# Moving the last weight preparations from GpSimd to VectorE around the start of the up-projection

## The chip, the cores and the metric

The kernel runs on one core of a Trainium2 chip. A core has five engines that work side by side, each through its own instructions in order: TensorE multiplies matrices (PE in the profile, PEld for its weight loads), VectorE (DVE) and GpSimd (POOL) do elementwise arithmetic, ScalarE (ACT) does activations and copies, and SyncE (SP) issues most DMA transfers; ScalarE and GpSimd can issue transfers too. On-chip memory is SBUF; TensorE writes its sums into the banks of PSUM. The metric is the device time of one execution in microseconds (us); lower is better.

## The reference

One layer of a decoder trunk on a sequence of 1024 rows of width 1024, in float32. Three branches (RWKV-7 time mixing, stick-breaking attention, cross-attention) are gated, summed and projected; a convolutional feed-forward block follows. Only the end of it matters here:

```python
branch_out = jnp.einsum('btnc,ncd->btnd', ys, w_branch[l])
gates = jax.nn.sigmoid(gate_logits.reshape(b, t, N_BRANCH, D_MODEL))
merged = jnp.sum(gates * branch_out, axis=2)
x = x + merged @ w_out[l]
x = x + conv_ffn(x, norm2_g[l], w_up[l], conv_w[l], conv_b[l], w_down[l])

def conv_ffn(x, g, w_up, conv_w, conv_b, w_down):
    h = rms_norm(x, g) @ w_up                      # 1024 -> 2 * 2816
    hp = jnp.pad(h, ((0, 0), (CONV_W - 1, 0), (0, 0)))
    acc = conv_b + hp[:, 0:t] * conv_w[0]
    for i in range(1, CONV_W):
        acc = acc + hp[:, i:i + t] * conv_w[i]     # causal, width 3
    gate, val = jnp.split(acc, 2, axis=-1)
    return (jax.nn.silu(gate) * val) @ w_down
```

## The kernel before, in words

**Split operands.** Each float32 operand x of a large product is split into a high part, which ScalarE writes by a rounding copy, and a low part x - high, written by an elementwise subtraction on VectorE or GpSimd. A product is then three matmuls: high by high, high by low, low by high. Whoever needs an operand waits for both parts.

**End of the branches and output projection.** `branch_last` computes the last branch in eight steps d of 128 output columns. In each, TensorE fills two PSUM banks, VectorE multiplies them by the gate (line 1230, which frees the banks), adds the sums of the other branches (line 1235), ScalarE writes the high parts `mg` (line 1241) and VectorE their low parts (line 1242). Then `out_proj` multiplies by the eight rows of tiles of the output weights, `wo[0]` to `wo[7]`, for eight blocks `tt` of 128 rows; blocks 0 and 1 run together, one k after the other. `load_wo(k)` loads and splits `wo[k]`: 0 to 3 inside `branch_last`, 4 to 7 at the start of `out_proj`, their low parts on GpSimd (line 85). The raw weights use two buffers `wr`, so `wo[6]` is loaded when `wo[4]` is split. In SBUF the parts of `wo[4]` are called `it` and `wo_sp`, those of 5 and 6 `qk`, of 7 `at`.

**Up-projection.** The activations are cut into four blocks of 512 by 512, and the product with the weights follows a scheme with seven products and sums of blocks in place of eight. The left operands, prepared once for all weights, are called 11 and 21 (`B` in the profile), 22 (also `B`), and T1 to T4 (`BT`). The weights come in pairs of 128-column tiles; pair 0 is a pair of gate columns, pair 1 the value columns that belong to it, and so on, 22 pairs. For pair n, product i (1 to 7) is 12 matmuls of 128x512 into one of four `mm` banks. The weights' operands are prepared per pair: `prep1` (products 1 and 2) from the first tile, `prep2` (5 and 6) from the sum s that `sums2` makes, `prep3` (7, 4 and 3) from the two that `sums3` makes. In the profile s is `it`, the raw tiles are `rw` (odd pairs) or `wr` (even ones), and the operands are `wh`, `wl` (high, low) and `l`. For pair 0 they come early, during the output projection (`wsec`, `wsum`, `wsh`, `wsl`). After the products VectorE combines the banks into `u`, and `conv` computes the convolution and the activation into `gall` (instructions on ScalarE and VectorE in turn), whose sums `act_sums` writes out for the down-projection.

**What sets the order.** A scheduler orders the instructions of an engine by priority and by what they wait for, and allots buffers; nothing moves once the program is built. `pinned` keeps instructions of one engine in the order of the code while `pin` is on; while `strict` is on too, each is also tied behind the pinned one before it. All matmuls are pinned. `behind(ins, prev)` ties one instruction behind another. In the up phase `strict` was off, and the order at its start is a list of calls: `step(n, i)` is product i of pair n, `hi` and `lo` write parts of left operands, `late(7)` transposes the last block of rows, `sums` makes the left operands' sums.

Of the kernel before, what the change touches and what calls it, by code (L numbers as in the profile page):

```python
# [12 lines left out]
F32 = mybir.dt.float32  # L13
# [8 lines left out]
C = 64  # L22
# [28 lines left out]
class Trunk:  # L51
# [30 lines left out]
    def split_raw(self, raw, hi, lo):  # L82
        ins = self.nc.scalar.activation(hi, raw, AF.Copy)  # L83
        self.behind(ins, self.last_fin)
        self.nc.gpsimd.tensor_tensor(lo, raw, hi.bitcast(F32), ALU.subtract)  # L85
        return hi, lo
# [1101 lines left out]
    def load_wo(self, k):  # L1188
        slots = ["qk"] * 4 + ["at"] * 4 + ["it", "sp"] + ["qk"] * 4 + ["at"] * 2
        hl = [self.pool_l.tile([128, 1024], F32R, name="wo_sp", tag="sp", bufs=1) if s == "sp" else self.t4(s, F32R) for s in slots[2 * k : 2 * k + 2]]  # L1190
        self.wo.append(self.split_raw(self.load_w(self.I["w_out"][k], self.last_go if k > 3 else None), *hl))
# [201 lines left out]
    def up_phase(self, raws, t2, operand, high, low, late, sums):  # L1393
# [13 lines left out]
        def load(n):  # L1407
            if n < len(pairs):
# [3 lines left out]
                for i in range(2):  # L1412
                    nc.sync.dma_start(W[n][i], self.I["w_up"][m + i])
# [10 lines left out]
        def prep1(n):  # L1424
            w = self.early[4 * n] if n < 2 else hl(W[n][0], self.pool_wt, ("wh", "wl"))
            st[n, 1], st[n, 2] = [[x[:, c] for x in w] for c in (L, R)]

        def sums2(n):
            keep = self.pinned if n == 1 else lambda ins: None
            w1, w2 = W[n]  # L1430
            s = st[n, "s"] = self.t4("it")
            keep(nc.gpsimd.tensor_tensor(s[:, L], w2[:, L], w2[:, R], ALU.add))
            keep(nc.gpsimd.tensor_tensor(s[:, R], s[:, L], w1[:, L], ALU.subtract))

        def sums3(n):
            keep = self.pinned if n == 1 else lambda ins: None
            w1, w2 = W[n]
            s4 = st[n, "s4"] = self.pool_r.tile([128, 552], F32, name=self.nm("s4"), tag="s4", bufs=1)[:, :512]
            keep(nc.gpsimd.tensor_tensor(w2[:, L], w1[:, L], w2[:, L], ALU.subtract))
            keep(nc.gpsimd.tensor_tensor(s4, w1[:, R], st[n, "s"][:, R], ALU.subtract))  # L1440

        def prep2(n):
            if n > 1:
                sums2(n)
            w = hl(st[n, "s"], self.pool_l, ("l4", "l4"), fixed=n < 2) if n else self.early[1]
            st[n, 5], st[n, 6] = [[x[:, c] for x in w] for c in (L, R)]

        def prep3(n):
            if n > 1:
                sums3(n)  # L1450
            w = hl(W[n][1] if n else self.early[2], self.pool_wt, ("wh", "wl"), fixed=n < 2, eng=nc.gpsimd if n else nc.vector)
            st[n, 7], st[n, 4] = [[x[:, c] for x in w] for c in (L, R)]
            if n:
                W.pop(n)
                del st[n, "s"]
                st[n, 3] = hl(st.pop((n, "s4")), self.pool_l, ("l4", "l4"), 512, n == 1)
# [23 lines left out]
        def conv_half(n, i, u, sg, h):  # L1480
            m = pairs[n][0] + i
            c = self.ps("g")
            nc.scalar.activation(c, u[:, 2 + h * 512 : 514 + h * 512], AF.Identity, scale=self.par("cw2", m), bias=self.par("cb", m))
            nc.vector.scalar_tensor_tensor(c, u[:, 1 + h * 512 : 513 + h * 512], self.par("cw1", m), c, ALU.mult, ALU.add)
            nc.vector.scalar_tensor_tensor(c, u[:, h * 512 : 512 + h * 512], self.par("cw0", m), c, ALU.mult, ALU.add)
            g = g_all[:, i * 2 + h]
            if not pairs[n][2]:
                nc.scalar.activation(sg[:, h], c, AF.Sigmoid)
                nc.vector.tensor_tensor(g, c, sg[:, h], ALU.mult)
            else:  # L1490
                nc.vector.tensor_tensor(g, c, g, ALU.mult)

        def conv(n, i, u):
            sg = None if pairs[n][2] else self.pool_l.tile([128, 2, 512], F32, name=self.nm("sg"), tag="sp", bufs=1)
            for h in range(2):
                conv_half(n, i, u, sg, h)
# [15 lines left out]
        def step(n, i):  # L1512
            if i == 1:
                A = st[n, "A"] = bank()
                product(n, 1, A, True, True)
                p1 = st[n, "p1"] = self.r4("p1", n=512)
                if n < 2:
                    self.pinned(nc.vector.tensor_copy(p1, A))  # L1518
                else:
                    nc.scalar.activation(p1, A, AF.Copy)  # L1520
# [8 lines left out]
            elif i == 6:  # L1529
# [5 lines left out]
                if n and pairs[n - 1][2]:  # L1535
                    act_sums(pairs[n - 1][1], True)
            elif i == 7:
# [8 lines left out]
                nc.vector.tensor_tensor(v[:, L2], Bk, st.pop((n, "p1")), ALU.add)  # L1546
                nc.vector.tensor_tensor(v[:, R2], st[n, "C"], v[:, L2], ALU.add)
# [13 lines left out]
            elif i == 3:  # L1561
# [6 lines left out]
                if n + 1 == len(pairs):  # L1568
                    conv(n, 1, st.pop((n, "u2")))
                conv(n, 0, u)  # L1570
# [13 lines left out]
        self.pin = True  # L1584
# [3 lines left out]
        step(0, 1)  # L1588
        sums2(1)
        hi("T1", old)  # L1590
        lo("T1", old)
        step(1, 1)
        sums3(1)
# [361 lines left out]
```

## Time and profile before

| | |
|---|---|
| time, median of 3 runs | 1824.77 us (1822.93 to 1825.58) |
| profiled execution, its own time | 1822.09 us |
| its span, first to last instruction | 1820.3 us |
| mean granted TensorE clock | 0.996 |
| output projection on TensorE | 1079.6 to 1177.4 us of the span |
| up-projection | from 1177.6 us |

A row of the timeline is: start in us, duration in us, engine, line, operation, out<-in, shape, a count where like instructions were merged, and in brackets the idle time of the engine ahead of it with what ended it. Merged instructions overlap a little, so two of 0.69 us each show as 1.3. A row of the waits is: engine and line that waited, engine and line waited for, us in total, times, the longest. In the answer by windows: stretch, its length, then busy us of PE, PEld, VectorE, ScalarE and GpSimd, the granted clock (1.00 is full), the DMA share and GB/s. In the groups by shape, the numbers after the bar are the busy us of all and the mean ns of one.

### The profile page before, as it was taken

Reading aid. Unit: us, or ns where it says so; the run is one execution under the profiler, and the core shown is the slowest. Engines: PE = TensorE matmul, PEld = TensorE weight load, DVE = VectorE, ACT = ScalarE, POOL = GpSimd, SP = SyncE. Lnnn points to the kernel's source line nnn. Section 1 sums busy time; section 2 is a strip of 40 time slices with the busy share of each in tenths; the row PEclk is TensorE's granted clock in tenths of the full one; section 3 lists DMA queues with packets and bytes.
Section 4 is the critical chain, followed back from the end, with each engine's and each line's share of the span. In section 5 each row is a group of like instructions: output and inputs, shape, how many; then the busy total and the mean of one; then the engine's idle time right before and its main releaser. Section 6 shows DMA issues by size and latency. Waiting matters only on the chain.

```text
span 1820.3 us, 27424 instructions
## 1 busy us (share of the span) xinstructions
PE 1784.4 (98%) x10468; PEld 1444.0 (79%) x10468; DVE 1191.1 (65%) x1659; ACT 882.7 (48%) x1665; POOL 770.1 (42%) x441
## 2 busy tenths in 40 slices
PE   8999999999999999999999999989999999999999
PEld 6777778878888888787777878868888888888887
DVE  5657773988977515232634792597776777786497
ACT  5443352555666645543556543464444444544343
POOL 2322343222221362221333341476777767645454
PEclk9999999999999999999999999999999999999999
DMA  4155466111112352457864562323332333386475
GB/s 182 59 174 185 146 191 221 50 42 50 58 41 79 103 162 65 154 190 243 283 230 182 204 213 105 127 61 113 110 110 87 101 114 110 122 298 240 145 236 203
DMA packets 120613, 263.39 MB, mean 145 GB/s; under 512 B 28313, under 2 KB 40857, under 8 KB 120354
## 3 DMA queue, kind: packets, MB, share of 16 engines
q1 hardware_dynamic: 82722, 194.76, 32.6%
q10 hardware_dynamic: 33984, 54.27, 8.1%
q0 software_dynamic: 3776, 12.62, 2.2%
q8 instruction: 82, 1.34, 0.3%
q14 instruction: 49, 0.40, 0.1%
HBM read 180.04 MB, written 81.53 MB: 144 GB/s over the span
## 4 chain that ended last, share of the span: by engine, by line
PE 77%; DVE 12%; issue 4%; ACT 3%; POOL 2%; DMA 2%; ACTq 0%; SPq 0%; DVEq 0%; POOLq 0%
PE mm L130 63%; PE g L130 11%; PE g L113 3%; POOL dw L1687 1%; DVE it L479 1%; DVE at L872 1%; DVE inst L481 1%; DVE qk L396 1%; DVE qk L398 1%; DVE BT L1328 1%; DVE w L774 0%; DVE qk L819 0%; DVE at L1235 0%; DMA w<-mrd 0%; DVE qk L606 0%
## 5 line engine op out<-in xcount | busy, mean ns | idle before, releaser
L85 POOL TENSOR_TENSOR wl<-wr,wh 128x1024 fp32r<-128x1024 f32 x77 | 195.7, 2542 | 443.5 <-ACT wh L83 437.0
L130 PE MATMUL mm<-xhi,wh 128*128 128x512 f32 x784 | 263.3, 416 | 8.3 <-ACT xhi L199 7.3
L130 PE MATMUL mm<-xlo,wh 128*128 128x512 f32 x784 | 245.5, 395 | 0.9 <-DVE xlo L200 0.9
L130 PE MATMUL mm<-xhi,wl 128*128 128x512 f32 x784 | 243.6, 392 | 0.0
L130 PEld LDWEIGHTS mm<-xlo,wh 128*128 128x128 f32 x784 | 148.2, 189 | 34.5 <-DVE xlo L200 1.6
L130 PEld LDWEIGHTS mm<-xhi,wl 128*128 128x128 f32 x784 | 147.9, 189 | 33.8 <-POOL wl L85 0.9
L130 PEld LDWEIGHTS mm<-xhi,wh 128*128 128x128 f32 x784 | 137.1, 190 | 38.3 <-issue 8.8
L83 ACT ACTIVATE wh<-wr 128x1024 fp32r<-128x1024 f32 x77 | 81.5, 1059 | 91.4 <-PE mm L130 51.3
L130 PE MATMUL mm<-dw,da 128*128 128x512 f32 x528 | 120.8, 390 | 0.0
L130 PE MATMUL mm<-BT,l 128*128 128x512 f32 x504 | 117.7, 389 | 0.0
L130 PEld LDWEIGHTS mm<-dw,da 128*128 128x128 f32 x528 | 98.9, 188 | 21.3 <-DVE da L1686 0.8
L1687 POOL TENSOR_TENSOR dw<-draw,dw 128x512 fp32r<-128x512 f32 x55 | 82.3, 1505 | 77.4 <-ACT dw L1685 75.9
L130 PE MATMUL mm<-BT,wh 128*128 128x512 f32 x352 | 109.2, 390 | 2.9 <-DVE BT L1328 2.9
L130 PEld LDWEIGHTS mm<-BT,l 128*128 128x128 f32 x504 | 94.6, 188 | 19.6
L130 PE MATMUL mm<-B,wh 128*128 128x512 f32 x352 | 108.6, 390 | 1.5 <-DVE p L1518 1.5
L872 DVE TENSOR_TENSOR_SCAN at<-at,at 128x128 f32<-128x128 f32 (+3 forms) x64 | 90.0, 1407 | 27.9 <-ACT at L866 27.7
L1686 DVE TENSOR_TENSOR da<-draw,da 128x512 fp32r<-128x512 f32 x77 | 70.6, 928 | 47.6 <-ACT da L1684 47.2
L1419 POOL TENSOR_TENSOR l<-it,l 128x1024 fp32r<-128x1024 f32 x21 | 51.6, 2457 | 95.5 <-ACT l L1418 95.5
L130 PE MATMUL g<-dw,da 128*128 128x512 f32 x396 | 90.5, 389 | 0.3 <-POOL dw L1687 0.3
L1684 ACT ACTIVATE da<-draw 128x512 fp32r<-128x512 f32 x77 | 48.3, 628 | 82.9 <-PE mm L130 32.0
L774 DVE TENSOR_TENSOR w<-w,rbc 128x1024 f32<-128x1024 f32 x24 | 50.5, 2105 | 58.0 <-ACT w L773 54.7
L186 POOL TENSOR_TENSOR hf<-rs,half 128x16 f32<-128x16 f32 (+1 forms) x18 | 48.9, 2718 | 91.1 <-DVE rs L183 86.4
(329 smaller groups left out, 4021.3 us busy)
## 6 DMA issues: line engine op xcount, KB each, us to landing
wr<-in_w_in_dram SPq DMA_DIRECT2D x50, 512.0 KB, 3.6
draw<-actd SPq DMA_DIRECT2D x77, 256.0 KB, 3.5
at<-scr SPq DMA_DIRECT2D x28, 512.0 KB, 5.4
draw<-in_w_down_dram SPq DMA_DIRECT2D x55, 256.0 KB, 4.7
rw<-in_w_up_dram SPq DMA_DIRECT2D x22, 512.0 KB, 3.5
actd<-gall ACTq DMA_DIRECT2D x44, 256.0 KB, 3.4
gsd<-w ACTq DMA_DIRECT2D x20, 512.0 KB, 2.8
wr<-in_w_up_dram SPq DMA_DIRECT2D x20, 512.0 KB, 3.7
```

Source lines behind the costliest of these rows:

```text
L83: ins = self.nc.scalar.activation(hi, raw, AF.Copy)
L85: self.nc.gpsimd.tensor_tensor(lo, raw, hi.bitcast(F32), ALU.subtract)
L113: self.pinned(self.nc.tensor.transpose(out, in_, self.ident[:n, :n]))
L130: self.pinned(self.nc.tensor.matmul(*a, **k))
L186: nc.gpsimd.tensor_tensor(out, t[:, :n], self.half[:, :n], ALU.pow)
L396: nc.vector.tensor_tensor(bk4[q, :, first ^ h2], self.c8(x[q, hs]), self.c8(Q[q, hs]), ALU.mult)
L774: nc.vector.tensor_tensor(g, g, self.rbc, ALU.mult)
L872: self.pinned(nc.vector.tensor_tensor_scan(sn[:, :W][:, ::-1], sn[:, :W][:, ::-1], self.smask[:, 1024 - W :][:, ::-1], 1.0, ALU.mult, ALU. ...
L1419: keep(eng.tensor_tensor(lo, src, hi.bitcast(F32), ALU.subtract))
L1684: self.pinned(nc.scalar.activation(A[:, 0], a, AF.Copy))
L1686: self.pinned(nc.vector.tensor_tensor(A[:, 1], a, A[:, 0].bitcast(F32), ALU.subtract))
L1687: nc.gpsimd.tensor_tensor(Wt[:, 1], w, Wt[:, 0].bitcast(F32), ALU.subtract)
```

## The change

Two things are changed, both between 1070 and 1250 us of the span.

*Output weights.* The low parts of `wo[4]` to `wo[7]` are written by VectorE, tied behind the last pinned VectorE instruction, that is behind the low parts of `branch_last`'s last step.

*Up phase up to the third pair.* `sums2`, `sums3` and the low parts of pairs 0 and 1 run on VectorE instead of GpSimd. The two copies `p` of product 1 out of PSUM run on ScalarE instead of VectorE. The low parts of T1, T3 and 22 are written in one instruction of 1024 elements per half instead of 768 and 256. Products of pair 2: product 1 stands ahead of product 3 of pair 1. Its raw weights are loaded by ScalarE's queue, behind the high part of s of pair 1, instead of SyncE's. The second convolution of pair 0 (on `u`), the convolutions of pair 1 and the sums of the first activations come later in the code, the two halves of pair 0's convolutions are interleaved, and the order up to pair 1's product 7 is strict.

The list of calls at the start of the up phase, and what it calls, from the diff:

```diff
-    def split_raw(self, raw, hi, lo):
+    def split_raw(self, raw, hi, lo, dve=False):
         ins = self.nc.scalar.activation(hi, raw, AF.Copy)
         self.behind(ins, self.last_fin)
-        self.nc.gpsimd.tensor_tensor(lo, raw, hi.bitcast(F32), ALU.subtract)
+        if dve:
+            ins = self.nc.vector.tensor_tensor(lo, raw, hi.bitcast(F32), ALU.subtract)
+            self.behind(ins, self.last_fixed[ins.ins.engine])
+        else:
+            self.nc.gpsimd.tensor_tensor(lo, raw, hi.bitcast(F32), ALU.subtract)
...
-        self.wo.append(self.split_raw(self.load_w(...), *hl))
+        self.wo.append(self.split_raw(self.load_w(...), *hl, k > 3))
...
-                    nc.sync.dma_start(W[n][i], self.I["w_up"][m + i])
+                    if n == 2:
+                        self.pinned(nc.scalar.dma_start(W[n][i], self.I["w_up"][m + i]))
+                    else:
+                        nc.sync.dma_start(W[n][i], self.I["w_up"][m + i])
...
+        def engine(n):
+            return self.pinned if n < 3 else lambda ins: None, nc.vector if n < 2 else nc.gpsimd
...
+                ins = nc.scalar.activation(p1, A, AF.Copy)
                 if n < 2:
-                    self.pinned(nc.vector.tensor_copy(p1, A))
...
-        self.pin = True
+        self.pin = self.strict = True
         load(1)
         prep1(0)
         prep1(1)
         step(0, 1)
+        step(1, 1)
         sums2(1)
-        hi("T1", old)
-        lo("T1", old)
-        step(1, 1)
-        sums3(1)
         late(7)
+        hi("T1", old)
...
+        prep2(1)
+        load(2)
         step(0, 7)
-        prep2(1)
+        sums3(1)
         u = step(0, 3)
-        prep3(1)
-        load(2)
         v = step(0, 4)
...
+                if n == 1 and i == 4:
+                    step(2, 1)
+                elif n == 2 and i == 6:
+                    conv(1, 0, u)
+                    act_sums(0, False)
+                elif n == 2 and i == 7:
+                    act_sums(0, True)
+                if n == 1 and i == 6:
+                    prep3(1)
+                    prep1(2)
+                    conv(0, 1, v)
+                elif n == 1 and i == 7:
+                    conv(0, 0, u)
+                    self.strict = False
```

VectorE where the output projection starts; `mg` are the last low parts of `branch_last`, `w<-mm,w` is the first sum of the output projection. Before:

```order
L1242 TENSOR_TENSOR mg_1_3_9599<-at_9897,mg_0_3_9595 128x512
L1242 TENSOR_TENSOR mg_1_0_1_9605<-at_9897,mg_0_0_1_9601 128x256
L1242 TENSOR_TENSOR mg_1_1_1_9607<-at_9897,mg_0_1_1_9603 128x256
L1276 TENSOR_TENSOR w_1653_10113<-mm_10007,w_1653_10113 128x512
L1276 TENSOR_TENSOR w_1653_10113<-mm_10008,w_1653_10113 128x512
```

After, in the changed kernel, whose lines are four further on here:

```order
L1246 TENSOR_TENSOR mg_1_3_9599<-at_9897,mg_0_3_9595 128x512
L1246 TENSOR_TENSOR mg_1_0_1_9605<-at_9897,mg_0_0_1_9601 128x256
L1246 TENSOR_TENSOR mg_1_1_1_9607<-at_9897,mg_0_1_1_9603 128x256
L86 TENSOR_TENSOR wo_sp<-wr_9978,it_9976 128x1024
L86 TENSOR_TENSOR qk_9983<-wr_9984,qk_9982 128x1024
L86 TENSOR_TENSOR qk_9989<-wr_9990,qk_9988 128x1024
L86 TENSOR_TENSOR at_9995<-wr_9996,at_9994 128x1024
L1280 TENSOR_TENSOR w_1653_10113<-mm_10007,w_1653_10113 128x512
```

The four low parts of the output weights stand between the two, where GpSimd had them at its own pace.

VectorE at the start of the up phase, from the sum of product 6 of pair 0 on (`BT...10724` is T3, `B...10728` is 22, the next `BT` T4). Before:

```order
L1534 TENSOR_TENSOR u_10825<-mm_10845,p_1728_10750 128x512
L1328 TENSOR_TENSOR BT_1_0_10726<-A_10001,BT_0_0_10724 128x2x384
L1328 TENSOR_TENSOR BT_1_1_10727<-A_10002,BT_0_1_10725 128x2x384
L1328 TENSOR_TENSOR BT_1_0_10726<-A_10001,BT_0_0_10724 128x2x128
L1328 TENSOR_TENSOR BT_1_1_10727<-A_10002,BT_0_1_10725 128x2x128
L1419 TENSOR_TENSOR wl_10864<-wsec_10509,wh_10863 128x1024
L1328 TENSOR_TENSOR B_1_0_10730<-A_10003,B_0_0_10728 128x1024
L1328 TENSOR_TENSOR B_1_1_10731<-A_10004,B_0_1_10729 128x1024
L1328 TENSOR_TENSOR BT_1_0_10873<-raw_10000,BT_0_0_10871 128x1024
L1328 TENSOR_TENSOR BT_1_1_10874<-raw_10000,BT_0_1_10872 128x1024
L1542 TENSOR_TENSOR u_10888<-mm_10845,p_1728_10750 128x512
```

After:

```order
L1546 TENSOR_TENSOR u_10820<-mm_10840,p_1728_10750 128x512
L1332 TENSOR_TENSOR BT_1_0_10726<-A_10001,BT_0_0_10724 128x1024
L1426 TENSOR_TENSOR wl_10856<-wsec_10509,wh_10855 128x1024
L1332 TENSOR_TENSOR BT_1_1_10727<-A_10002,BT_0_1_10725 128x1024
L1332 TENSOR_TENSOR B_1_0_10730<-A_10003,B_0_0_10728 128x1024
L1426 TENSOR_TENSOR l_1742_10880<-wsum_10510,l_1741_10879 128x512
L1332 TENSOR_TENSOR B_1_1_10731<-A_10004,B_0_1_10729 128x1024
L1332 TENSOR_TENSOR BT_1_0_10886<-raw_10000,BT_0_0_10884 128x1024
L1332 TENSOR_TENSOR BT_1_1_10887<-raw_10000,BT_0_1_10885 128x1024
L1426 TENSOR_TENSOR l_1744_10893<-it_10767,l_1743_10892 128x1024
L1554 TENSOR_TENSOR u_10876<-mm_10840,p_1728_10750 128x512
```

Two low parts `l` have joined from GpSimd, and `wl` stands between the halves of T3; further on (not shown) follow `sums3` of pair 1 and its two last low parts.

GpSimd at the start of the up phase (`rs` is the last row norm). Before:

```order
L186 TENSOR_TENSOR rs_1723_10707<-rs_10710,half 128x1
L1432 TENSOR_TENSOR it_10752<-rw_10734 128x512
L1433 TENSOR_TENSOR it_10752<-it_10752,rw_10733 128x512
L1439 TENSOR_TENSOR rw_10734<-rw_10733,rw_10734 128x512
L1440 TENSOR_TENSOR s_1732_10774<-rw_10733,it_10752 128x512
L1419 TENSOR_TENSOR l_1743_10892<-wsum_10510,l_1742_10891 128x512
L1419 TENSOR_TENSOR l_1745_10914<-it_10752,l_1744_10913 128x1024
L1419 TENSOR_TENSOR wl_10931<-rw_10734,wh_10930 128x1024
L1432 TENSOR_TENSOR it_11013<-wr_10939 128x512
```

After:

```order
L190 TENSOR_TENSOR rs_1723_10707<-rs_10710,half 128x1
L1426 TENSOR_TENSOR wl_10967<-wr_10896,wh_10966 128x1024
L1442 TENSOR_TENSOR it_11000<-wr_10897 128x512
L1443 TENSOR_TENSOR it_11000<-it_11000,wr_10896 128x512
L1426 TENSOR_TENSOR l_1764_11004<-it_11000,l_1763_11003 128x1024
L1449 TENSOR_TENSOR wr_10897<-wr_10896,wr_10897 128x512
```

GpSimd's first instruction of the up phase is now the low part `wl` of pair 2, and the eight that belonged to pairs 0 and 1 are gone.

92 lines of the change are left out of this document (49 added, 43 removed).

## The prediction

> **What bounds the kernel now.** I read the busy times first, then who TensorE waited for, then the timeline at each of those waits.
>
> ```profile
> PE 1784.4 (98%) x10468; PEld 1444.0 (79%) x10468; DVE 1191.1 (65%) x1659; ACT 882.7 (48%) x1665; POOL 770.1 (42%) x441
> ```
>
> TensorE is the bound over the whole. The same number of matmuls stays, so only its gaps can be won. Its waits from 960 to 1250 us, which holds all the change touches, but for one of 0.5 us in the branches:
>
> ```profile
> PE mm L130 <- DVE BT L1328: 2.9, 2, 1.7
> PE mm L130 <- DVE at L1230: 2.3, 1, 2.3
> PE mm L130 <- DVE p L1518: 1.5, 1, 1.5
> PE mm L130 <- DVE u L1547: 1.1, 1, 1.1
> PE mm L130 <- DVE wl L1419: 1.0, 1, 1.0
> ```
>
> Together 8.8 us, all ended by VectorE. Behind them TensorE has no gap to take a gain back:
>
> ```profile
> 1235.00:1300.00 65.00, 65.00 (x289) 53.83 (x288) 44.20 (x67) 31.22 (x43) 49.79 (x30) 1.00 0.28 94
> 1300.00:1400.00 100.00, 100.00 (x443) 82.84 (x442) 77.85 (x115) 47.23 (x65) 73.63 (x43) 1.00 0.35 115
> ```
>
> TensorE is busy for 65 of 65 and 100 of 100 us, GpSimd for about three quarters, so what is won ahead of 1235 us reaches the end unless GpSimd or VectorE falls behind there.
>
> **Gap one, where the output projection starts.** The timeline of three engines:
>
> ```profile
> 1076.34 2.40 POOL L85 TENSOR_TENSOR wo_sp<-wr,it 128x1024 fp32r<-128x1024 f32 x1 [9.56 <-ACT it L83]
> 1076.60 4.95 DVE L1242 TENSOR_TENSOR mg<-at,mg 128x256 fp32r<-128x256 f32 x2 [0.55 <-ACT mg L1241]
> 1078.70 2.56 POOL L85 TENSOR_TENSOR qk<-wr,qk 128x1024 fp32r<-128x1024 f32 x1
> 1079.63 1.52 PE L130 MATMUL mm<-qk,mg 128*128 128x512 f32 x6
> 1082.68 1.28 DVE L1230 TENSOR_TENSOR at<-mm,at 128x512 f32<-128x512 f32 x2
> 1083.41 6.34 PE L130 MATMUL mm<-qk,mg 128*128 128x512 f32 x18 [2.26 <-DVE at L1230]
> 1089.60 5.60 PE L130 MATMUL mm<-at,mg 128*128 128x512 f32 x24
> ...
> L1328 DVE TENSOR_TENSOR BT<-t,BT 128x256 fp32r<-128x256 f32 x2 | 0.8, 423 | 0.1
> ```
>
> Two subtractions of 256 elements took 4.95 us where the last row has 0.42 us for each: they end with GpSimd's two subtractions `wo_sp` and `qk` (1078.7 and 1081.3). An instruction of VectorE that reads two operands from SBUF has waited here for a whole one of GpSimd, twice. Behind them stand the sums (1.3 us) and then the gate product of line 1230 that frees the banks for block 1. TensorE sat idle for 2.26 us.
>
> It cost more than that. 24 matmuls take 5.60 us in the last PE row, a pitch of (5.60 - 0.39) / 23 = 0.227 us with 0.39 us for the last one. The 18 behind the gap lasted from 1083.41 to 1089.60, 6.19 us, where 18 x 0.227 = 4.08: 2.11 us more, since the granted clock fell to one half.
>
> ```profile
> 1085.00:1087.00 2.00, 2.00 (x6) 1.62 (x5) 2.00 (x1) 1.06 (x1) 2.00 (x1) 0.50 0.00 0
> ```
>
> The clock took its price here after a gap of 2.26 us. [...]
>
> **Gap two, the start of the up phase.**
>
> ```profile
> 1183.03 0.86 PEld L113 LDWEIGHTS g<-kon,sq 128*128 128x128 f32 x8 [0.25 <-ACT sq L1286]
> 1183.75 3.94 DVE L1328 TENSOR_TENSOR BT<-raw,BT 128x768 fp32r<-128x768 f32 x2 [0.77 <-ACT BT L1323]
> 1188.35 0.73 PE L130 MATMUL mm<-B,wh 128*128 128x512 f32 x2 [1.47 <-DVE p L1518]
> 1197.13 1.22 DVE L1419 TENSOR_TENSOR wl<-wsec,wh 128x1024 fp32r<-128x1024 f32 x1
> 1198.41 0.51 PE L130 MATMUL mm<-BT,wl 128*128 128x512 f32 x1 [0.97 <-DVE wl L1419]
> 1200.95 3.03 POOL L1419 TENSOR_TENSOR l<-it,l 128x1024 fp32r<-128x1024 f32 x1 [1.44 <-ACT l L1418]
> 1201.65 6.74 DVE L1328 TENSOR_TENSOR BT<-raw,BT 128x1024 fp32r<-128x1024 f32 x2
> 1203.94 3.37 POOL L1419 TENSOR_TENSOR wl<-rw,wh 128x1024 fp32r<-128x1024 f32 x1
> 1205.12 0.50 PE L130 MATMUL mm<-BT,wh 128*128 128x512 f32 x1 [1.20 <-DVE BT L1328]
> 1208.44 0.50 PE L130 MATMUL mm<-BT,wh 128*128 128x512 f32 x1 [1.67 <-DVE BT L1328]
> 1221.85 2.97 PE L130 MATMUL mm<-B,l 128*128 128x512 f32 x12 [1.08 <-DVE u L1547]
> ```
>
> VectorE's two 1024-element parts of T4 took 6.74 us under two of GpSimd's, against 1.22 us for one alone (`wl`): some 4.3 us of blocking, of which 1.20 and 1.67 us reach TensorE. The copy `p` queued behind two blocked parts of T1 cost 1.47 us. With the transposes' 0.25 the six waits are 0.25 + 1.47 + 0.97 + 1.20 + 1.67 + 1.08 = 6.64 us. Each restart also shows a first matmul of 0.50 us or so instead of 0.39, another 0.1.
>
> **The change, part by part.**
>
> *Output weights' low parts.* Four instructions of 1.22 us join VectorE behind the last `mg` parts. Without GpSimd the two blocked parts end near 1077.4, the sums near 1078.7, and the gate product waits for TensorE's last branch matmul (about 1079.6), not TensorE for it: banks come free near 1080.3 and 1080.9, and TensorE has its first six matmuls until 1081.0. The gap goes, and the half clock with it: 2.26 + 2.11 = 4.4 us (lower bound 0, if the gate product waits for another thing). By the same durations the parts of `wo[4]` and `wo[5]` end near 1086.2 and 1087.3; TensorE reaches them at 1079.6 + 48 x 0.227 = 1090.5 and 1093.2. Then `wo[6]` and `wo[7]` are loaded into their buffers.
>
> ```profile
> wr<-in_w_up_dram SPq DMA_DIRECT2D x20, 512.0 KB, 3.7
> L1418 ACT ACTIVATE wh<-rw 128x1024 fp32r<-128x1024 f32 x3 | 3.2, 1058 | 3.6 <-PE mm L130 3.6
> L1520 ACT ACTIVATE p<-mm 128x512 f32<-128x512 f32 x2 | 1.2, 592 | 0.4 <-PE mm L130 0.4
> L1556 DVE TENSOR_TENSOR u<-u,mm 128x512 f32<-128x512 f32 x3 | 2.1, 689 | 1.5 <-PE mm L130 1.3
> L1484 DVE SCALAR_TENSOR_TENSOR g<-u,params,g 128x512 f32<-128x512 f32 x12 | 8.7, 752 | 2.6 <-ACT g L1483 2.6
> L1433 POOL TENSOR_TENSOR it<-it,rw 128x512 f32<-128x512 f32 x2 | 2.6, 1290 | 0.2
> L1419 POOL TENSOR_TENSOR wl<-wr,wh 128x1024 fp32r<-128x1024 f32 x2 | 4.8, 2411 | 0.0
> 1226.75 0.92 ACTq L1505 DMA_DIRECT2D actd<-gall  x2
> ```
>
> 3.7 us of load, 1.06 of ScalarE and 1.22 of VectorE put `wo[7]` at 1087.3 + 6.0 = 1093.3, asked for at 1098.7. Hidden by 4 to 5 us; the sums of block 0 queued behind them on VectorE are due after 1105.
>
> *Copies `p` on ScalarE.* 0.59 us each, at 1183.0 when the last row norm's copy is done: 1183.6 and 1184.2. Product 2 of pair 0 asks after the transposes (1184.1), that of pair 1 at 1186.8. The 1.47 us go.
>
> *Sums and low parts of pairs 0 and 1 on VectorE.* VectorE takes on eight instructions, six of 512 elements and two of 1024: 6 x 0.69 + 2 x 1.22 = 6.6 us. It sheds 4.3 us of blocking at T4, some 2 at T1 (3.94 against 2 x 0.95 for 768 elements, an estimate from 1.22 for 1024), and two copies. Back to back an instruction costs 0.08 us less than its duration (two of 0.68 show as 1.28): 1.14 for 1024, 0.61 for 512, 0.34 for 256. TensorE, at 12 x 0.227 = 2.72 us a product from 1184.1, starts products 6, 5 and 7 of pair 0 at 1189.5, 1192.3 and 1195.0. VectorE is free of the transposes' copies and four sums near 1187.9 (1184.2, ScalarE's copies out of the first bank, four of VectorE's, four sums at 0.34, T2's high parts; an estimate), and needs 6 x 0.34 + 2 x 1.14 = 4.3 us: 1192.2. Then `u` of product 6, half of T3 and `wl`: 1192.3 + 0.61 + 1.14 + 1.22 = 1195.3, asked for by the third matmul at 1195.45. The rest follows in step: first half of 22 near 1197.5 (asked 1197.9), `l` 1198.2 (1198.2), T4 1200.5 (1200.7), `l` of pair 1 1202.8 (1203.7). VectorE paces TensorE for 8 us with margins of 0 to 1 us. I leave 0.5 us of waits there (bounds 0 and 2) and the 0.25 of the transposes: 6.64 - 0.75 = 5.9 us gained, and 0.4 of restarts.
>
> *Load of pair 2 by ScalarE.* Two issues of some 0.5 us at about 1200 instead of SyncE at 1192; landed by 1205. Queued behind them is the high part of pair 1's `rw`, which waits for `sums3` on VectorE (1205.6) anyhow: nothing. SyncE's queue loses two entries that nothing waited behind.
>
> *Product 1 of pair 2 ahead, convolutions back.* By TensorE's 2.72 us a product it stands at 1214.0; `wh` is written near 1208.4 and GpSimd's `wl` ends at 1210.9. Product 3 of pair 1, which waited 1.08 us for VectorE, now comes at 1216.8, and its bank is read near 1214 (1208.7, four convolution steps, four sums): that wait is in the sum above. But GpSimd has begun no earlier and TensorE is 6 us ahead. To the `wl` of pair 3's product 1 GpSimd has five of 2.41 and twelve of 1.29 us, 27.5, and about 1.1 for ScalarE's part between: 1208.5 + 28.7 = 1237.2. TensorE asks at 1233.1 + 2.72 + 0.45 = 1236.3. VectorE has, from 1208.7 to the sum that frees the bank for product 3 of pair 2, sixteen convolution steps of 0.67 and seventeen of 0.61: 21.1 us, 1229.8, asked for at 1233.1. But it can be blocked again:
>
> ```profile
> 1232.05 1.42 DVE L1500 TENSOR_TENSOR gall<-gall 128x512 f32<-128x512 f32 x2
> 1233.99 2.94 POOL L1419 TENSOR_TENSOR l<-it,l 128x1024 fp32r<-128x1024 f32 x1 [5.06 <-ACT l L1418]
> 1233.99 3.49 DVE L1500 TENSOR_TENSOR gall<-gall 128x512 f32<-128x512 f32 x2
> ```
>
> The activations' sums cost 1.42 us free and 3.49 under GpSimd, 2.1 more; the last `l` of pair 1 meets GpSimd's first `wl` and can lose 2.4. 4.5 - 3.3 of slack is 1.2 us of new wait, which covers GpSimd's 0.9. Bounds: 0 and 4.5.
>
> Sum: 4.4 + 5.9 + 0.4 - 1.2 = 9.5 us. Against the profiled execution, 1822.09 us, that is 1812.6; it ran 2.7 us below the median, which I keep: 1824.77 - 9.5 = **1815.3 us**.
>
> **Rivals.**
>
> - *VectorE starts its chain late.* ScalarE's copies and high parts ahead of T2 are in strict order too; 2 us late there reach TensorE whole, and as one gap of over 2 us bring the half clock (2.1). For it: margins of 0 to 1 us. Against: GpSimd is idle then. 9.5 - 4.1 = 5.4 us, 1819.4.
> - *GpSimd blocks VectorE around pair 2*, the whole 4.5 us reaching TensorE: 9.5 - 3.3 = 6.2, 1818.6.
> - *Gap one stays*: the gate product waits for its operands, not for GpSimd; against it, VectorE went from the blocked parts to the sums and the product with no idle time. 5.1 us, 1819.7.
> - *Two of these together*: 1 to 3 us left, 1822.5, no change that can be told.
> - *Slower.* Pair 2's weights now hang on VectorE: ScalarE writes `wh` of pair 2 only behind two high parts that wait for `sums3`, and GpSimd's 28.7 us follow. That chain already ends 0.9 us after TensorE asks, so each us that `sums3` ends after 1206 is one on TensorE. It decides the sign from 9.5 us on; 11 us late with the half clock give 1828.4. Against it: from 1187.9 VectorE has 18 us of counted work without GpSimd.
>
> **How the numbers follow.** 0.2% (3.6 us) is about what a measurement of this kernel tells from no change. Chances: forecast 0.56, late VectorE 0.17, GpSimd's blocking 0.08, gap one 0.06 (all faster, 0.87), two together 0.08 (same), slower 0.05. Low end: every wait gone, 4.4 + 6.6 + 0.6 = 11.6, and 1 us of the runs' spread: 1812.0. High end: past the three single rivals, 1820.5.
>
> **What would show it.** No gap and no clock below 1.00 at the start of the output projection; no wait for `p`, T4 or `u`; VectorE's parts there at 0.42 and 1.22 us; waits for VectorE or GpSimd of 1 to 2 us in pairs 2 and 3; TensorE's busy time as before. Wrong, if VectorE idles between the transposes and T4 behind ScalarE, or if GpSimd's first `wl` of pair 2 starts after 1210 us less the gain of gap one.

## The result and the profile after

The changed kernel took 1815.51 us (median; 1815.13 to 1817.16), the kernel before 1825.17 us beside it: a ratio of 0.9947, 95% interval 0.993 to 0.9964, so 9.7 us less (6.6 to 12.8). The forecast was 1815.3 us. The sum came out; not every term of it did.

The profiled spans are 1820.3 and 1813.6 us, 6.7 apart, and part of that lies ahead of the change: TensorE reached the output projection at 1079.63 us before and at 1080.79 after, though nothing up to there was changed; that start moves from one execution to the next (last section). Kernels are therefore compared by two stretches: from the first matmul of the output projection (`mm<-qk,mg`) to the first product of the up phase (`mm<-B,wh`), and from there to the end of the span. The timeline of TensorE, before and then after:

```profile
1177.60 0.62 PE L130 MATMUL mm<-B,wh 128*128 128x512 f32 x2
```

```profile
1080.79 5.65 PE L134 MATMUL mm<-qk,mg 128*128 128x512 f32 x24
...
1174.27 0.62 PE L134 MATMUL mm<-B,wh 128*128 128x512 f32 x2
```

Before: 1177.60 - 1079.63 = 97.97 us and 1820.3 - 1177.60 = 642.7. After: 93.48 and 639.3. The first stretch gave 4.5 us, the second 3.4, together 7.9.

**Gap one is gone.** ScalarE's and VectorE's timeline after, at the place where TensorE had waited 2.26 us:

```profile
1077.66 1.06 ACT L83 ACTIVATE it<-wr 128x1024 fp32r<-128x1024 f32 x1 [3.30 <-DMA wr<-in_w_out_dram]
1079.06 0.76 DVE L1246 TENSOR_TENSOR mg<-at,mg 128x256 fp32r<-128x256 f32 x2 [1.86 <-ACT mg L1245]
1080.95 1.28 DVE L1234 TENSOR_TENSOR at<-mm,at 128x512 f32<-128x512 f32 x2
1086.08 1.22 DVE L86 TENSOR_TENSOR wo_sp<-wr,it 128x1024 fp32r<-128x1024 f32 x1
```

The two parts of `mg` take 0.76 us where they took 4.95; the 24 matmuls from 1080.79 run in 5.65 us with no gap. VectorE now waits 1.86 us there for ScalarE. The cause is a load: on ScalarE the high part of `wo[4]` (`it`) stands ahead of `mg` and waits for it, 3.30 us here and 2.26 us before; that the change has a part in this is not shown. It ate the margin that the forecast had seen. In the kernels below with the same code the wait of VectorE lies between 0.75 and 2.28 us, and the two with over 2.2 us took 6.1 and 6.0 us for these 24 matmuls.

**Five of the six waits of gap two are gone.** TensorE's waits after, from 960 to 1300 us, by line (total, times, longest):

```profile
PE mm L134 <- DVE u L1560: 2.0, 1, 2.0
PE mm L134 <- DVE u L1485: 0.8, 1, 0.8
PE g L134 <- DVE ys L551: 0.5, 1, 0.5
PE mm L134 <- POOL wl L1426: 0.3, 1, 0.3
```

None of the lines of before stands there but the 0.5 us of the branches. The sixth wait, 0.25 us of a weight load at the transposes, has stayed (timeline of the weight loads after):

```profile
1179.69 0.85 PEld L117 LDWEIGHTS g<-kon,sq 128*128 128x128 f32 x8 [0.24 <-ACT sq L1290]
```

In place of the five are three new waits of 2.0 + 0.8 + 0.3 = 3.1 us, all for pairs 2 and 3. The timeline of VectorE, GpSimd and TensorE in the up phase after:

```profile
1195.90 2.35 DVE L1332 TENSOR_TENSOR BT<-raw,BT 128x1024 fp32r<-128x1024 f32 x2
...
1204.42 2.62 POOL L1426 TENSOR_TENSOR wl<-wr,wh 128x1024 fp32r<-128x1024 f32 x1 [25.98 <-ACT wh L1425]
1204.71 2.89 DVE L1426 TENSOR_TENSOR l<-s,l 128x512 fp32r<-128x512 f32 x1
...
1226.02 2.39 POOL L1426 TENSOR_TENSOR l<-it,l 128x1024 fp32r<-128x1024 f32 x1
1226.84 3.81 DVE L1513 TENSOR_TENSOR gall<-gall 128x512 f32<-128x512 f32 x2
1231.30 0.69 DVE L1560 TENSOR_TENSOR u<-mm,u 128x512 f32<-128x512 f32 x1
1231.91 4.46 DVE L1513 TENSOR_TENSOR gall<-gall 128x512 f32<-128x512 f32 x2
1232.14 3.00 PE L134 MATMUL mm<-B,l 128*128 128x512 f32 x12 [2.01 <-DVE u L1560]
```

T4 takes 2.35 us in place of 6.74, since GpSimd is idle until 1204.42. From its first instruction on the old pattern is back: the last `l` of pair 1 takes 2.89 us in place of 0.69, and the first pair of activation sums 3.81 in place of 1.42. The sum that frees the bank (`u`, line 1560) stands behind them, and TensorE waits 2.01 us for it. After 1250 us TensorE has no room to take anything back, as before:

```profile
1250.00:1300.00 50.00, 50.00 (x223) 41.39 (x222) 37.27 (x56) 22.69 (x31) 36.50 (x22) 1.00 0.34 111
1300.00:1500.00 200.00, 200.00 (x884) 165.63 (x883) 149.73 (x222) 91.22 (x123) 144.71 (x84) 1.00 0.31 102
```

### The profile page after: what moved, and what is told of

It is laid out like the page before. It is cut to its first block, busy times and chain, and to the rows that moved or that the text cites. A ratio compares the mean times of both kernels' runs of the same rounds, so it can differ in the third digit from the quotient of the medians.

```text
span 1813.6 us, 27412 instructions
## 1 busy us (share of the span) xinstructions
PE 1781.2 (98%) x10468; PEld 1442.2 (80%) x10468; DVE 1188.7 (66%) x1665; ACT 882.0 (49%) x1667; POOL 746.4 (41%) x429
## 4 chain that ended last, share of the span: by engine, by line
PE 67%; DVE 9%; issue 2%; ACT 2%; POOL 2%; DMA 0%; ACTq 0%; SPq 0%; POOLq 0%; DVEq 0%
PE mm L134 56%; PE g L134 9%; PE g L117 2%; POOL dw L1715 1%; DVE it L483 1%; DVE at L876 1%; DVE inst L485 1%; DVE gall L1513 1%; DVE gall L1502 0%; DVE g L1497 0%; DVE qk L823 0%; DVE g L1496 0%; ACT at L1095 0%; DVE qk L822 0%; DVE w L778 0%
## 5 line engine op out<-in xcount | busy, mean ns | idle before, releaser
L134 PEld LDWEIGHTS g<-dw,da 128*128 128x128 f32 x396 | 74.3, 188 | 16.2 <-POOL dw L1715 0.8
```

The lines of the kernel that those rows point to most:

```text
L134: self.pinned(self.nc.tensor.matmul(*a, **k))
```

## The experiments

All in one table: median, ratio to the kernel before on the same chip with its 95% interval, and the two stretches of the profiled execution. The intervals are some 3.5 to 6.6 us wide; the stretches, which leave out the work upstream, tell smaller differences, though from one execution each: kernels with the same code in a stretch, gap one apart, differ by up to 0.5 us in the first and 0.4 us in the second, and less than that says nothing.

| kernel | median us | ratio | projection to up phase | up phase to end |
|---|---|---|---|---|
| before | | | 97.97 | 642.7 |
| after | 1815.51 | 0.9947 (0.9930-0.9964) | 93.48 | 639.3 |
| output weights only | 1817.44 | 0.9962 (0.9950-0.9974) | 93.52 | 643.1 |
| up phase only | 1821.87 | 0.9982 (0.9972-0.9992) | 96.22 | 639.4 |
| before, GpSimd in pieces there | 1820.69 | 0.9982 (0.9972-0.9991) | 94.10 | 642.7 |
| order without the engine | 1817.53 | 0.9954 (0.9942-0.9966) | 93.48 | 640.4 |
| engine without the order | 1820.77 | 0.9977 (0.9968-0.9987) | 98.74 | 640.2 |
| sums behind product 7 | 1817.56 | 0.9959 (0.9947-0.9972) | 93.95 | 640.1 |
| load by SyncE | 1814.23 | 0.9945 (0.9930-0.9961) | 93.49 | 639.1 |
| product 1 back | 1815.02 | 0.9947 (0.9933-0.9960) | 93.52 | 639.1 |
| copies on VectorE | 1816.67 | 0.9954 (0.9941-0.9968) | 93.49 | 639.3 |
| pairs 3, 4 in pieces | 1816.88 | 0.9957 (0.9942-0.9972) | 93.50 | 640.9 |
| pieces, load by SyncE | 1816.35 | 0.9953 (0.9935-0.9971) | 93.85 | 638.1 |
| pieces, low part first | 1813.53 | 0.9939 (0.9926-0.9953) | 93.69 | 636.9 |

### Is gap one GpSimd's doing?

Three kernels: the first part of the change alone, the rest alone, and the kernel before with GpSimd's four instructions cut.

```diff
 # output weights only: before, with
-self.nc.gpsimd.tensor_tensor(lo, raw, hi.bitcast(F32), ALU.subtract)
+if dve:   # wo[4] to wo[7]
+    ins = self.nc.vector.tensor_tensor(lo, raw, hi.bitcast(F32), ALU.subtract)
+    self.behind(ins, self.last_fixed[ins.ins.engine])
...
 # up phase only: after, with
-..., *hl, k > 3))
+..., *hl, False))
 # pieces: before, with
-self.nc.gpsimd.tensor_tensor(lo, raw, hi.bitcast(F32), ALU.subtract)
+for j in range(4):    # wo[4] to wo[7], 256 elements each
+    c = slice(j * 256, (j + 1) * 256)
+    self.nc.gpsimd.tensor_tensor(lo[:, c], raw[:, c], hi.bitcast(F32)[:, c], ALU.subtract)
```

> The kernel before with the first part of the change alone: low parts of wo[4] to wo[7] on VectorE. Blocking theory (VectorE's two parts of 256 elements waited for whole GpSimd instructions): no TensorE wait for line 1230's product, clock 1.00 at the start of the output projection, the six waits of the up phase (6.6 us) as before; 4.4 us less than before, ratio 0.9976. Rival (the gate product waits for loads or for ScalarE's high parts): the gap stays at 2 us or so and the time is that of before.

> The changed kernel with the low parts of wo[4] to wo[7] back on GpSimd, so the up phase's part alone. If the parts add up: the gap of some 2.3 us with the half clock behind it is back (VectorE's two parts of 256 at 5 us), the up phase is as in the changed kernel (waits of 3.1 us at pairs 2 and 3, none for p, T4, or product 3 of pair 1); 4.1 us less than before, ratio 0.9977, and 4.4 more than the changed kernel. Rival (one part makes up for the other, so that either alone gives most of the gain): within 2 us of the changed kernel.

> The kernel before; GpSimd keeps the low parts of wo[4] to wo[7] but writes each in four instructions of 256 elements instead of one of 1024. Whole-instruction theory (VectorE waits until GpSimd's instruction that runs ends, not longer): each blocked part of VectorE waits at most one piece of about 0.7 us, so the two take at most 2.2 us instead of 4.95, the gap of 2.26 us falls to 0.3 or less and the clock stays at 1.00; about 4 us less than before, ratio 0.9978. Rival (the two engines share the bandwidth, each slowed while both work): the two parts stay near 5 us and the time is that of before.

The first part alone gives 4.45 us in its stretch (97.97 - 93.52) and loses 0.4 in the other; its six waits of gap two all stand. The median puts it at 4.7 to 9.1 us, a little over the 4.4 forecast; the runs differ upstream by more than that excess (the output projection began between 1078.05 and 1082.88 us in these kernels). Without it, the up phase keeps its 3.3 us and gap one is back, 2.03 us long; by the medians this kernel is 2.6 us below the one before (1.5 to 5.1), where 4.1 had been expected. Its profiled execution is the shortest of its twelve and has no half clock behind the gap. GpSimd and VectorE in the kernel before with pieces:

```profile
1077.02 3.64 POOL L88 TENSOR_TENSOR wo_sp<-wr,it 128x256 fp32r<-128x256 f32 x4 [8.52 <-ACT it L83]
1077.28 1.64 DVE L1245 TENSOR_TENSOR mg<-at,mg 128x256 fp32r<-128x256 f32 x2 [0.46 <-ACT mg L1244]
```

GpSimd does the same work beside the same two instructions of VectorE, and they take 1.64 us in place of 4.95. Gap one goes, 3.9 of the 4.5 us with it. So VectorE waits here for about one instruction of GpSimd at a time: 2.5 us for an instruction of 0.42 beside GpSimd's of 2.40 and 2.56 us, 0.82 us beside pieces of 0.91 us (3.64 / 4). It is their length that costs, not GpSimd's work.

### The order or the engine?

In the up phase the change moves the sums and low parts of pairs 0 and 1 to VectorE and writes the steps in another order. Each was tried without the other. The kernel with the order alone keeps the output weights on VectorE and the copies `p` on ScalarE; the kernel with the engine alone has neither.

```diff
 # order without the engine: after, with
-return self.pinned if n < 3 else lambda ins: None, nc.vector if n < 2 else nc.gpsimd
+return self.pinned if n < 3 else lambda ins: None, nc.gpsimd
-st[0, 3] = hl(..., 512, True, nc.vector)
+st[0, 3] = hl(..., 512, True)
...     # wl of pair 0 stays on VectorE, as in the kernel before
 # engine without the order: before, with
+def engine(n): return nc.vector if n < 2 else nc.gpsimd
-keep(nc.gpsimd.tensor_tensor(...))     # sums2, sums3, low parts of pairs 0, 1
+keep(engine(n).tensor_tensor(...))
...
```

> The changed kernel with the sums and the eight low parts of pairs 0 and 1 back on GpSimd, in the changed order, with the copies p on ScalarE and the output weights on VectorE. Blocking theory: VectorE's parts of T1, 22 and T4 take up to 3.4 us each again instead of 1.2, TensorE waits 2 to 5 us between products 5 of pair 0 and 6 of pair 1; 3 us more than the changed kernel, ratio to before 0.9963. Rival (the order and the copies p gave the up phase's gain): within 1 us of the changed kernel, ratio 0.9947.

> The kernel before with one part of the change alone: sums and low parts of pairs 0 and 1 on VectorE in place of GpSimd, at the places where they stood; the order, the copies, the second pair's convolutions and the output weights as before. From the first up product to pair 3's product 1 the kernel before takes 65.88 us, the changed kernel 60.71, and the changed kernel with this part undone 62.00. Theory (the order brings most of the gain and the engine a smaller share): 64 to 65.5 us, a total of 0.5 to 2 us under the kernel before; the blocked instructions on T4 (6.74 us) fall to 2.35, but VectorE does the sums ahead of T1 and is later there. Rival 1 (the engine brings all of it): 61 to 62 us, a total 4 to 5 us under. Rival 2 (without the order the added work on VectorE only delays it): 66 to 69 us, a total 0 to 3 us over.

From the first up product to product 1 of pair 3 it takes 66.10 us before (1243.70 - 1177.60; the 65.88 of the expectation is too small), 61.98 with the order alone, 62.77 with the engine alone (1239.56 - 1176.79) and 60.71 with both. Each alone brings more than half: 4.1 and 3.3 of 5.4 us. None of the theories for the second kernel held; it landed between the theory and the first rival. With the engine alone the waits for `p` and T4 are gone (4.3 us together); the 0.97 us for `wl` stay, 0.64 us for a left operand's parts are new, and product 3 of pair 1 waits 1.52 us in place of 1.08. With the new order as well, none of these three is there. With the order alone, T4 is blocked again, and this shows on TensorE:

```profile
PE mm L134 <- DVE BT L1332: 2.0, 2, 1.5
PE mm L134 <- DVE u L1485: 0.8, 1, 0.8
PE mm L134 <- DVE B L1332: 0.5, 1, 0.5
```

```profile
1194.27 5.64 DVE L1332 TENSOR_TENSOR BT<-raw,BT 128x1024 fp32r<-128x1024 f32 x2
```

Waits of 1.46 + 0.57 + 0.54 = 2.6 us are back in pair 0 (products 3 and 4), yet up to product 1 of pair 3 the kernel loses 1.3 us and to the end 1.1. The 2.01 us at pair 2's product 3 are missing: TensorE, held up earlier, comes there when VectorE is done. What TensorE loses early it does not wait for late, as long as VectorE's queue, and not TensorE, sets the time of that product.

### What of the small parts?

```diff
 # load by SyncE: after, with
-if n == 2: self.pinned(nc.scalar.dma_start(W[n][i], ...))
+nc.sync.dma_start(W[n][i], ...)
 # product 1 back: after, with
-step(2, 1)      # behind product 4 of pair 1
+order of pair 2: (1, 5, 6, 2, 7, 4, 3)
 # copies on VectorE: after, with
-ins = nc.scalar.activation(p1, A, AF.Copy)
+self.pinned(nc.vector.tensor_copy(p1, A))    # pairs 0, 1
```

> The changed kernel with pair 2's raw weights loaded by SyncE's queue, as before. Predicted price of ScalarE's two issues: nothing, so the same time within 1 us. Rival (the load's later landing sets when GpSimd starts on pair 2): GpSimd's first wl of pair 2 starts earlier and the waits at pairs 2 and 3 shrink.

> The changed kernel with product 1 of pair 2 behind product 3 of pair 1, as before. Theory (VectorE reads the bank of product 3 of pair 1 in time either way now): if that bank is read by 1213.2 us, TensorE reaches the product 2.7 us earlier, at 1210.9, and waits 2.3 us there; 0 to 2 us more than the changed kernel. Rival (moving the product gave nothing): same within 0.5 us.

> The changed kernel with the two copies p on VectorE, as before. Theory (VectorE paces this stretch with margins under 1 us): two copies of 0.61 us put its chain 1.2 us later; TensorE waits 0.5 to 1.5 us for it at products 7 and 3 of pair 0; 1 us more than the changed kernel. Rival (only the blocked parts ahead of the copy made it late): same within 0.3 us.

All three lie within 0.2 us of the changed kernel from the up phase to the end, and no ratio tells them from it. With the load by SyncE and with the copies on VectorE the wait stays where it was (timelines of TensorE in the two kernels):

```profile
1231.26 4.58 PE L134 MATMUL mm<-B,l 128*128 128x512 f32 x12 [2.04 <-DVE u L1557]
```

```profile
1234.28 4.57 PE L134 MATMUL mm<-B,l 128*128 128x512 f32 x12 [2.02 <-DVE u L1561]
```

With product 1 put back, product 3 of pair 1 waits instead, and pair 2's does not:

```profile
1212.81 3.01 PE L134 MATMUL mm<-B,l 128*128 128x512 f32 x12 [2.25 <-DVE u L1560]
```

So moving that product shifted a wait of 2 us by one pair and won nothing. With the copies on VectorE no wait for `p` comes back, and the kernel with the engine alone, whose copies are on VectorE, has none either: GpSimd's absence is enough to take those 1.47 us away. With the order alone, GpSimd is back, the copies are on ScalarE, and no such wait shows; whether the copies' move alone would do it was not tried.

### Where does the new wait come from?

First the activation sums were taken out from ahead of the sum that TensorE waits for; then GpSimd's instructions beside them were shortened.

```diff
 # sums behind product 7: after, with
-    conv(1, 0, u)
-    act_sums(0, False)
-elif n == 2 and i == 7:
-    act_sums(0, True)
+    conv(1, 0, u)
+elif n == 2 and i == 7:
+    act_sums(0, False)
+    act_sums(0, True)
 # pairs 3, 4 in pieces: after; GpSimd's sums and low parts beside these sums
-keep(eng.tensor_tensor(lo, src, hi.bitcast(F32), ALU.subtract))
+for c in parts(n):     # slices of 256 elements
+    keep(eng.tensor_tensor(lo[:, c], src[:, c], hi.bitcast(F32)[:, c], ALU.subtract))
...     # and the sums in the same way
```

> The changed kernel with the first pair's activation sums (four VectorE instructions, blocked by GpSimd) all behind the two sums u of pair 2's product 7, instead of two ahead of them. Theory (those two, 3.81 us under GpSimd, hold up the sum that frees the bank for product 3 of pair 2): the wait of 2.01 us goes; the one of 0.85 us at pair 3 may stay; 2 us less than the changed kernel. Rival (VectorE is simply behind by then, whatever the order): a wait of 1 us or more stays at the same place or moves to the next bank, same time.

> The changed kernel, with GpSimd's work for pairs 3 and 4 that stands beside the activation sums (sums for two products, low part of the sums, low part of the first weights) cut into pieces of 256 elements; nothing else moves. Theory (GpSimd's whole instructions hold VectorE up): the first pair of activation sums takes 2.4 to 2.8 us in place of 3.81, TensorE's wait at pair 2's product 3 shrinks from 2.01 to 0.6-1.0 us, and from the first up product to pair 3's product 1 it takes 59.3 to 59.9 us in place of 60.71; about 1 us less than the changed kernel in all. Rival (VectorE simply has too much to do there, whoever shares with it): the first pair stays at 3.6 to 3.8 us and the wait at 1.8 to 2.2. A second rival: the pieces let VectorE in between so often that GpSimd's low part for pair 3 comes late, and the wait moves there, as it did when the sums were put behind product 7: 1 to 2 us at that place, no gain.

With the sums put behind, the 2.01 us went and 2.68 us came, one product later, for GpSimd's low part of pair 3:

```profile
1229.20 7.70 DVE L1513 TENSOR_TENSOR gall<-gall 128x512 f32<-128x512 f32 x4
1233.57 5.58 POOL L1426 TENSOR_TENSOR wl<-rw,wh 128x1024 fp32r<-128x1024 f32 x2
...
1236.40 0.50 PE L134 MATMUL mm<-B,wl 128*128 128x512 f32 x1 [2.68 <-POOL wl L1426]
```

Four sums take 7.70 us beside GpSimd, 1.9 us each, where the shortest in the kernel before takes 0.68. Cut into pieces:

```profile
1224.74 1.91 DVE L1524 TENSOR_TENSOR gall<-gall 128x512 f32<-128x512 f32 x2
1227.90 1.83 DVE L1524 TENSOR_TENSOR gall<-gall 128x512 f32<-128x512 f32 x2
1233.05 5.14 POOL L1427 TENSOR_TENSOR wl<-rw,wh 128x256 fp32r<-128x256 f32 x5
1233.83 0.50 PE L134 MATMUL mm<-B,wl 128*128 128x512 f32 x1 [2.27 <-POOL wl L1427]
```

3.81 and 4.46 us become 1.91 and 1.83, less than the theory had asked for, and product 3 of pair 2 starts without a wait. But the second rival came true as well: TensorE stops 2.27 us for the low part of pair 3. Nothing was won. That wait was not a lack of GpSimd's time; ScalarE's timeline in this kernel has the high part ready ten microseconds before:

```profile
1222.39 1.07 ACT L1425 ACTIVATE wh<-rw 128x1024 fp32r<-128x1024 f32 x1 [1.57 <-PE mm L134]
```

GpSimd did the sums of pair 4 in between, 1228.03 to 1233.05. Two last kernels: the pieces with the load by SyncE, and the pieces with pair 4's sums put behind pair 3's low part.

```diff
 # pieces, low part first: pairs 3, 4 in pieces, with, in sums2(4)
 ins = eng.tensor_tensor(s[:, a], w2[:, a], w2[:, b], ALU.add)
+self.behind(ins, self.low3)     # pair 3's first low part
```

> The changed kernel with GpSimd's work for pairs 3 and 4 in pieces of 256 elements and pair 2's raw weights loaded by SyncE's queue. Theory: the two edits add: 1 to 2 us less than the changed kernel, a ratio of 0.9940 to the kernel before, if the wait at pair 2's product 3 falls under 1 us and no half clock follows it. Rival (a gap of 2 us costs 2 us or 3.7 with the half clock behind it, whichever way it falls): the wait stays at 2 us and the total lies within 1.5 us of the changed kernel's on either side.

> As the kernel with pairs 3 and 4 in pieces of 256 elements, and GpSimd makes pair 3's first low part ahead of pair 4's sums in place of behind them; no other instruction moves on any engine. In that kernel ScalarE had the high part ready at 1223.5 us, GpSimd started the low part at 1233.05, behind 5.0 us of pair 4's sums, and TensorE waited 2.27 us for it. Theory (that wait was a place in GpSimd's queue, not a lack of time): the low part starts some 56 us after the first up product in place of 60.9, TensorE waits 0 to 0.5 us there, and the product with it starts 59.4 to 59.9 us after the first up product in place of 61.67. Total 1.5 to 2.3 us under the changed kernel, ratio to the kernel before 0.9935 to 0.9945. Rival (the up phase is held by the sum of what VectorE and GpSimd have to do; a wait that is removed comes back further on): a new wait of 1.5 to 2.5 us at pair 3's later products, and the total within 0.7 us of the changed kernel's.

The load changed nothing at that place (a wait of 2.26 us for the same low part, at 1237.49). The order of GpSimd's queue did. Low part first, all three engines:

```profile
1228.15 1.92 DVE L1528 TENSOR_TENSOR gall<-gall 128x512 f32<-128x512 f32 x2
1231.33 3.73 POOL L1427 TENSOR_TENSOR wl<-rw,wh 128x256 fp32r<-128x256 f32 x4
1231.56 3.00 PE L134 MATMUL mm<-B,l 128*128 128x512 f32 x12
1234.85 0.39 PE L134 MATMUL mm<-B,wl 128*128 128x512 f32 x1
```

Product 3 of pair 2 starts in step with the matmuls ahead, the low part's matmul follows 59.29 us after the first up product (61.67 in the kernel it was made from), and from 1200 to 1250 us TensorE is busy but for 0.2 us:

```profile
1200.00:1250.00 50.00, 49.78 (x218) 40.58 (x217) 44.61 (x67) 25.70 (x36) 41.76 (x36) 1.00 0.31 101
```

It was the shortest of all, 1813.53 us, ratio 0.9939 (0.9926 to 0.9953), and 2.4 us shorter than the changed kernel from the up phase to the end. The two ratios' intervals overlap, so that it beats the changed kernel is shown by the waits of the profile, not yet by the times.

## Why the prediction was right, and where it was not

- *Gap one, 4.4 us:* right in place, cause and size (4.5 in its stretch). The load of `wo[4]`, on which ScalarE's `mg` hangs, was no term of it; it took most of the margin. The same gap without the half clock behind it, in the kernel with the up phase only, cost 96.22 - 93.48 = 2.7 us. The forecast took the 2.11 us of half clock for a fixed price; behind the 2.03 us of gap one in that kernel no half clock came (last section).
- *Gap two, 5.9 + 0.4 us:* five waits went whole, 6.39 us. The 0.25 us left for the transposes stayed; the 0.5 left for VectorE's tight chain did not appear. Its margins of 0 to 1 us held, though only just: at 1192.02 us a weight load waited 0.30 us for `wl`, and the matmuls show no idle time for it.
- *Copies `p`, "the 1.47 us go":* the wait went, but the copies were not needed for it. This step is wrong in its cause as far as it gives the gain to the copies; the idle GpSimd brings it anyhow.
- *Load of pair 2, nothing:* right, within 0.2 us.
- *Product 1 moved ahead, and the new wait of 1.2 us:* the mechanism was right (activation sums and the last `l` of pair 1 under GpSimd), the term too small. The blockings measured 2.5 us at the sums (3.81 against 1.28, two free instructions) and 2.2 at `l`, 4.7 where 4.5 was the bound. The slack set against them, 3.3 us, was too generous: TensorE asked near the forecast time (1230.13 us, which is 1233.46 counted from the start of the up phase as before, against 1233.1), but VectorE's sum ended at 1231.99 (1235.32), 0.8 us later than the 1229.8 and 4.7 us of blocking make, and product 3 waited 2.01. "Covers GpSimd's 0.9" failed also: pair 3's low part brought 0.28 us of its own, and product 7 of pair 3 another 0.85 that no step had. New waits: 3.1 us in place of 1.2.
- *The rivals:* GpSimd's blocking around pair 2 came in part, 2.01 of its 4.5 us reaching TensorE at product 3; the others did not come. GpSimd's first `wl` of pair 2 began at 1204.42, which is 1204.42 + 1177.60 - 1174.27 = 1207.75 on the time axis of before, 2.2 us ahead of the 1210; `sums3` ended at 1202.38 (1205.71), ahead of the 1206 from which that rival counts, so the slower case was never near.

The waits of the profile make 4.5 + 6.4 - 3.1 = 7.8 us, the two stretches 7.9; the medians' 9.7 hold upstream differences besides. The forecast's 9.5 put the new waits 1.9 too low and the gain at each of the gaps 0.1 too low (4.5 against 4.4, and 6.4 of waits against 5.9 and 0.4 of restarts). With the 7.9 us of the stretches it would have been 1816.9 us; that 1815.3 met the median to 0.2 us is partly luck. The low end of the range adds up to 1812.2, not 1812.0 us; nothing hangs on it.

## What to carry to other kernels

Where VectorE waits for a whole instruction of GpSimd, shorten that instruction: GpSimd's work cut into 256 elements freed VectorE nearly as well at gap one as moving it did (3.9 of 4.5 us), and puts no work on VectorE; GpSimd took 3.64 us in place of 2.40 for one low part. When a wait is removed, ask which queue sets the next one, and look whether the late instruction waits for data or only for its turn; three edits here moved a wait of some 2 us about, and the order of one queue removed it. Compare edits of a few microseconds by the stretch they touch, between two landmarks in the trace.

## What was not expected of the hardware

A gap of some 2 us has no fixed price here: gap one cost 4.5 us where half clock followed (2.26 us long, kernel before) and 2.7 us where none did (2.03 us, up phase only). In the kernel before, half clock began at 309.82, 617.02 and 1084.65 us, among others (the granted clock is the third number from the right; 0.82 over half a microsecond at one half is a start at 309.82):

```profile
309.50:310.00 0.50, 0.50 (x2) 0.46 (x3) 0.50 (x1) 0.50 (x1) 0.50 (x1) 0.82 0.00 0
617.00:617.50 0.50, 0.50 (x2) 0.39 (x2) 0.46 (x1) 0.50 (x2) 0.34 (x1) 0.52 0.00 0
1084.50:1085.00 0.50, 0.50 (x4) 0.36 (x3) 0.50 (x3) 0.00 (x0) 0.46 (x1) 0.65 0.00 0
```

The distances are 307.20 = 90 x 3.4133 and 467.63 = 137 x 3.4134 us. So half clock begins on a grid of 3.413 us here. All 40 stretches at half clock between the start and the end of the 14 profiles last one cell of it, 3.41 us. In the one at 1084.65 us eight matmuls of `mm<-qk,mg` begin, most of 0.63 us, where at full clock they take 0.39 and 3.41 / 0.227 = 15 would begin; half of a cell (granted clock 0.50), 1.7 us, is the price. The cell that holds the gap and the next one, in the kernel before, in the changed one and in the one with the load by SyncE:

```profile
1081.24:1084.65 3.41, 1.15 (x4) 0.74 (x5) 3.41 (x7) 2.27 (x4) 0.14 (x2) 1.00 0.69 202
1084.65:1088.06 3.41, 3.41 (x10) 2.67 (x9) 3.41 (x4) 1.07 (x2) 3.00 (x2) 0.50 0.00 0
```

```profile
1230.27:1233.68 3.41, 1.54 (x7) 1.31 (x8) 3.38 (x6) 0.77 (x1) 3.41 (x3) 1.00 0.02 5
1233.68:1237.09 3.41, 3.13 (x14) 2.27 (x13) 3.41 (x3) 0.00 (x0) 3.41 (x2) 1.00 0.29 24
```

```profile
1228.25:1231.66 3.41, 1.37 (x7) 0.86 (x6) 3.38 (x5) 1.06 (x1) 3.33 (x3) 1.00 0.00 0
1231.66:1235.07 3.41, 3.41 (x10) 2.63 (x9) 3.41 (x2) 0.00 (x0) 3.41 (x3) 0.50 0.02 5
```

TensorE idle for 3.41 - 1.37 = 2.04 us of a cell was followed by half clock, 1.87 us was not, with gaps of 2.04 and 2.01 us. The other gaps of about 2 us and more between 1070 and 1250 us fit: 2.02, 2.26, 2.27 and 2.68 us inside one cell were, gaps of 2.03, 2.07, 2.25 and 2.26 us that a border of the grid cut were not. One does not fit: with the engine alone the gap of 2.91 us left 1.70 us of idle time in its second cell, and half clock followed. Further up in the kernel before, idle time fails as the measure altogether; half clock followed both of these cells:

```profile
149.40:152.81 3.41, 1.66 (x19) 1.48 (x19) 3.37 (x6) 1.15 (x1) 0.00 (x0) 1.00 0.81 273
306.41:309.82 3.41, 3.41 (x71) 2.90 (x70) 1.62 (x4) 2.57 (x4) 0.48 (x1) 1.00 0.02 5
```

The first has 1.75 us of idle time, the second none, but 64 of its 71 matmuls are of 2 or 4 columns, where a cell of the up phase holds 15 of 512. What sets half clock off is open.

The half clock also hides what follows: behind it the 0.28 and 0.85 us of waits of the changed kernel are missing in the kernels with the load by SyncE and with the copies on VectorE, so these lost 1.7 us and got 1.1 back. Their second stretch is no longer than the changed kernel's all the same; the 0.6 us between are not accounted for. Between the two kernels in pieces with the old queue the second stretch differs by 2.8 us; the half clock (1.7) and a wait of 0.3 us in a later pair account for 2.0, and 0.8 us stay open.

Half clock also makes much of the spread between executions, which the stretches compared above leave out. Ahead of the output projection the 14 profiles have one to four such stretches; the four with one reached it at 1078.05 to 1078.97 us, the three with four at 1081.87 to 1082.88. Of the twelve executions of the kernel with the up phase only, the shortest took 1816.67 us at a mean granted clock of 0.998, the longest 1824.44 us at 0.994: 0.004 of 1820 us is 7.3 of the 7.8 us between them.
